# Z and gate columns of the second token half as seven block products on pairs of units

## The chip, the cores and the metric

The kernel runs on one core of one Trainium2 chip. The time is the device time of one execution in microseconds; three executions of a kernel give a median. A profile of one further execution gives the spans of all instructions and transfers. Engines are named as in the profile: PE (TensorE), DVE (VectorE), ACT (ScalarE), POOL (GpSimd), and SP (SyncE), which issues nearly all DMA transfers.

## What is computed

One hybrid decoder layer for 2048 tokens of 1024 channels: RMS norm, one input projection to 9224 columns, a gated DeltaNet branch and a dilated sliding-window attention branch, each with a SiLU gate path (the z columns), per-channel sigmoid gates, an output projection and the residual. Cut to what matters here:

```python
h = rms_norm(x, norm_w)
proj = h @ w_in                                  # (2048, 1024) @ (1024, 9224)
(dn_qkv, dn_z, dn_b, dn_a, swa_q, swa_k, swa_v, swa_z, gates) = split(proj)
o_dn  = rms_norm(delta_net(dn_qkv, dn_a, dn_b)) * silu(dn_z)      # 4 heads x 128
o_swa = merge(attention(swa_q, swa_k, swa_v)) * silu(swa_z)       # 4 heads x 128
g_dn, g_swa = split(gates)                                        # 2 x 1024
merged = sigmoid(g_dn) * (o_dn @ w_branch_dn) + sigmoid(g_swa) * (o_swa @ w_branch_swa)
out = x + merged @ w_out
```

The change concerns `swa_z` (512 columns) and `gates` (2048 columns) of `proj`.

## The kernel before

**Arithmetic.** Each float32 operand of a large product is split into a high part (rounded to fp32r, a copy on ScalarE) and a low part (the rest, a subtraction), and a product is three matmuls: high x high, high x low, low x high (`split`, line 86). The normalised input is held so in `hh` and `hl`, [128, 4, 8, 512]: four slots n of 512 tokens, eight slices k of 128 channels.

**First stage: attention columns.** The 4608 attention columns are computed for one token half (1024 tokens) at a time in 16 units (`unit`, line 413): units 0 to 7 for the first half, 8 to 15 for the second. A unit is a 2x2x2 block product (halves of the tokens, of the channels, of the unit's columns) done with seven block products in place of eight: `PROD` lists them, with the operand of x, the accumulator, whether it opens it, and the operand of w. The operands of x are the four blocks A11, A12, A21, A22 of the half and four sums of them: S1 = A21 + A22, S2 = S1 - A11, S3 = A11 - A21, S4 = A12 - S2; those of w are B11 to B22 and T1 = B12 - B11, T2 = B22 - T1, T3 = B22 - B12, T4 = T2 - B21. `SLOT` says where an operand of x stands: A11 to A22 of the half at hand in slots 2 and 3, the sums in slots 0 and 1. `save` and `restore` move an operand (high and low, 1 MB each) between its slot and the DRAM scratch `opd`; A11, A12 and A22 of the first half are saved in units 1 to 3, and during unit 15 the four blocks of the first half are loaded over the sums (`HOME`), so that afterwards `hh`, `hl` hold all 2048 tokens. The split w operands of the first half are written to `wdr` and read back for the second half. Attention runs meanwhile, a step every three or four hooks.

**Column blocks.** Then come 36 units of 128 columns each (`ccols`, line 1292): three z units of DeltaNet, twelve q, k, v units of DeltaNet, five z units (one of DeltaNet, four of `swa_z`), sixteen gate units. `cunits` (707) goes through them; for each it takes the four token slots n in turn, 24 matmuls of 128x512 into one bank of PSUM (three are there, `mm`), and gives the result to the unit's function: `z_block` (1145: tanh on ScalarE, a multiply on VectorE, store to `zscr`), `g_block` (1152: tanh, store to `gscr`) or a DeltaNet block. `c_load` (689) and `c_part` (703) fetch and split the next unit's w: high on ScalarE, low on GpSimd. The tiles `gt` of the z and gate functions are two.

**Work in the background.** `hook` (673) is called every six of these matmuls; `at(d, fn)` (670) puts a piece of work d hooks later. Pieces put there run beside the column blocks: after the first three units `open_dn` (1337); in unit 15, nine hooks in, `start_inverse` (1346): 63 rows of a triangular inverse on VectorE (`inverse`, 997; row i is one product of i x i elements, line 1020, and one reduction, 1023), each a number of hooks after the one before; then the store of the result, `scan` (1027; 16 steps of three hooks, with small matmuls on TensorE, each waiting for work of VectorE and ScalarE), then `start_fin` (1356: loads and merging of the attention outputs, `combine` 1186, and `o_prep` 1215). In the last unit, ahead of slot 2, `tail` (1377) starts loading and splitting the weights of the output projections into slots 0 and 1 of `hh`, `hl`.

**Order.** From `open_dn` to `start_inverse`, and all through the first stage, the order on PE, ACT, DVE and POOL is that of the program text (`manual_schedule`, line 1279); SP's is not, and elsewhere no engine's is: there a planner orders each engine's queue when the kernel is built, by its own estimate of when each instruction is ready, earlier ones in the text first. On the chip each queue is worked through in that order.

```python
PROD = (("A11", "a", True, "B11"), ("S2", "b", True, "T2"), ("A12", "a", False, "B21"), ("S3", "b", False, "T3"),
        ("S1", "c", True, "T1"), ("A22", "b", False, "T4"), ("S4", "c", False, "B22"))
SLOT = {"A11": (2, 0), "A12": (2, 1), "A21": (3, 0), "A22": (3, 1), "S1": (0, 0), "S2": (0, 1), "S3": (1, 0), "S4": (1, 1)}
```

## Time and profile before

| | |
|---|---|
| time, median of 3 runs | 2352.74 us (2350.87 to 2353.64) |
| the profiled execution | 2357.82 us |
| its span, first to last instruction | 2356.0 us |
| mean granted TensorE clock | 0.990 |
| DMA traffic | 452.23 MB, mean 192 GB/s |

How to read the profile: "busy" is the time in which an engine has at least one instruction running. Matmuls overlap, so the mean length of one in a group is longer than the distance between two; the distance comes from a count over a window in which TensorE does nothing else. A row of a group gives line, engine, operation, names written and read, shapes and count, then busy us and the mean ns of one, then the engine's idle time just before such instructions and who ended it. A row of a timeline gives start and length in us, and in brackets the idle time before it. A row of the chain gives start and length of a piece of the work that ended last. A row of DMA issues gives count, size and the median us from issue to landing. A row of windows gives for each stretch its length, each engine's busy us with the count, the granted clock, the DMA share and GB/s.

### The profile page before, as it was taken

The numbers are of one execution on the slowest core, as the hardware profiler recorded it, in microseconds if no ns is written. First come the engines' busy times: TensorE is split into PE (matmuls) and PEld (weight loads), VectorE is DVE, ScalarE is ACT, GpSimd is POOL, SyncE is SP. The second block draws the span as 40 slices with busy tenths as digits, with TensorE's granted clock in tenths as the row PEclk, the third lists the DMA queues.
The fourth block names the chain that finished last, engine by engine and source line by source line (L and its number), as shares of the span: only waits on it lengthen the run. The fifth ranks groups of instructions, "written<-read, shape, count | busy, mean of one in ns | idle before, by whom it ended". The sixth has DMA issues, their size and how long they took to land.

```text
span 2356.0 us, 43344 instructions
## 1 busy us (share of the span) xinstructions
PE 2297.1 (97%) x15216; PEld 2086.2 (89%) x15216; DVE 1347.7 (57%) x2853; ACT 907.2 (39%) x2948; POOL 889.2 (38%) x1331
## 2 busy tenths in 40 slices
PE   7999999979999999999999999999999999999999
PEld 7999999879999999888787888888888788889988
DVE  6566576594435535445777767999244423444431
ACT  5345466653324435445666651111233214111110
POOL 5374266574403303402675561111232213433442
PEclk8999999999999999999999999999999999999999
DMA  9989889857887888853544443222677636554542
GB/s 296 325 277 323 272 283 292 269 161 239 251 265 236 246 273 261 259 148 101 130 110 132 127 103 113 72 76 69 212 207 208 193 120 175 161 179 150 148 139 77
DMA packets 525969, 452.23 MB, mean 192 GB/s; under 512 B 66168, under 2 KB 490424, under 8 KB 523320
## 3 DMA queue, kind: packets, MB, share of 16 engines
q1 hardware_dynamic: 525464, 449.39, 62.6%
q8 instruction: 121, 1.98, 0.3%
q14 instruction: 96, 0.79, 0.1%
q10 hardware_dynamic: 288, 0.07, 0.0%
HBM read 263.45 MB, written 185.89 MB: 191 GB/s over the span
## 4 chain that ended last, share of the span: by engine, by line
PE 66%; DMA 5%; DVE 3%; POOL 1%; ACT 1%; issue 1%; SPq 0%; DVEq 0%; POOLq 0%; ACTq 0%
PE mm L433 12%; PE mm L720 10%; PE mm L721 10%; PE mm L722 10%; PE mm L1254 2%; PE mm L1256 2%; PE mm L1255 2%; PE mm L1237 2%; PE mm L1239 2%; PE mm L1238 2%; DMA oscr<-ol 2%; DMA gcb<-gcscr 1%; PE tp L584 1%; PE po L626 1%; DMA raw<-in_w_out_dram 1%; PE tp L617 1%
## 5 line engine op out<-in xcount | busy, mean ns | idle before, releaser
L720 PE MATMUL mm<-hh,w 128*128 128x512 f32 x1152 | 463.3, 402 | 0.0
L722 PE MATMUL mm<-hh,w 128*128 128x512 f32 x1152 | 457.8, 397 | 0.0
L721 PE MATMUL mm<-hl,w 128*128 128x512 f32 x1152 | 456.9, 397 | 0.0
L433 PE MATMUL mm<-w,hh 128*128 128x256 f32 x1760 | 328.3, 286 | 0.0
L433 PEld LDWEIGHTS mm<-w,hh 128*128 128x128 f32 x1760 | 271.2, 190 | 0.0
L88 POOL TENSOR_TENSOR w<-raw,w 128x512 fp32r<-128x512 f32 x68 | 100.0, 1472 | 435.0 <-ACT w L87 434.8
L720 PEld LDWEIGHTS mm<-hh,w 128*128 128x128 f32 x1152 | 220.3, 191 | 45.9
L722 PEld LDWEIGHTS mm<-hh,w 128*128 128x128 f32 x1152 | 217.0, 188 | 46.9
L433 PE MATMUL mm<-hh 128*128 128x256 f32 x880 | 257.5, 293 | 0.0
L721 PEld LDWEIGHTS mm<-hl,w 128*128 128x128 f32 x1152 | 217.6, 189 | 42.4
L433 PE MATMUL mm<-hl,hh 128*128 128x256 f32 x880 | 249.8, 284 | 0.9 <-POOL hl L295 0.9
L433 PE MATMUL mm<-hh,hl 128*128 128x256 f32 x880 | 249.6, 284 | 0.0
L433 PE MATMUL mm<-w,hl 128*128 128x256 f32 x880 | 248.3, 282 | 0.0
L607 DVE CUSTOM_DVE_ANT_0 p<-sc,mask 128x128 f32<-128x128 f32 (+1 forms) x192 | 70.0, 365 | 213.8 <-PE sc L604 87.0
L433 PEld LDWEIGHTS mm<-hl,hh 128*128 128x128 f32 x880 | 169.4, 192 | 1.3 <-POOL hl L295 1.3
L433 PEld LDWEIGHTS mm<-hh 128*128 128x128 f32 x880 | 169.3, 192 | 0.0
L433 PEld LDWEIGHTS mm<-hh,hl 128*128 128x128 f32 x880 | 169.0, 192 | 0.0
L433 PEld LDWEIGHTS mm<-w,hl 128*128 128x128 f32 x880 | 166.1, 189 | 0.0
L368 POOL TENSOR_SCALAR st<-st 128x4 f32<-128x4 f32 x96 | 21.1, 219 | 374.0 <-ACT junk L367 371.9
L1237 PE MATMUL mm<-oh,hh 128*128 128x256 f32 x512 | 143.7, 281 | 1.7 <-DVE gt L1241 1.7
L1239 PE MATMUL mm<-oh,hl 128*128 128x256 f32 x512 | 142.9, 279 | 0.0
L1238 PE MATMUL mm<-ol,hh 128*128 128x256 f32 x512 | 142.9, 279 | 0.0
(304 smaller groups left out, 5492.1 us busy)
## 6 DMA issues: line engine op xcount, KB each, us to landing
wdr<-w SPq DMA_DIRECT2D x56, 512.0 KB, 4.8
w<-wdr SPq DMA_DIRECT2D x54, 512.0 KB, 5.1
qk<-qks SPq DMA_DIRECT2D x212, 128.0 KB, 3.9
qks<-rec SPq DMA_DIRECT2D x96, 256.0 KB, 3.2
raw<-in_w_in_dram SPq DMA_DIRECT2D x68, 256.0 KB, 3.3
gscr<-gt SPq DMA_DIRECT2D x64, 256.0 KB, 2.5
gt<-gscr SPq DMA_DIRECT2D x64, 256.0 KB, 3.4
wdr<-hh SPq DMA_DIRECT2D x28, 512.0 KB, 4.4
```

Of the source, the lines that this page charges most:

```text
L88: eng.tensor_tensor(out=l, in0=raw, in1=h.bitcast(F32), op=ALU.subtract)
L433: mm = lambda x, y, **kw: nc.tensor.matmul(o, x, y, skip_group_check=True, **kw)
L607: nc.vector.tensor_tensor_reduce(out=p[:, lo:hi], in0=sc[:, lo:hi], in1=self.mask[:, slot * P + lo:slot * P + hi], scalar=3e38, scale=-SCA ...
L720: nc.tensor.matmul(pr, wh[:, k, :], a, start=(k == 0), stop=False)
L721: nc.tensor.matmul(pr, wh[:, k, :], b, start=False, stop=False)
L722: nc.tensor.matmul(pr, wl[:, k, :], a, start=False, stop=(k == KT - 1))
L1237: nc.tensor.matmul(o, self.wbh[:, k, ms], oh[:, k, :], start=(k == b * 4), stop=False)
L1238: nc.tensor.matmul(o, self.wbh[:, k, ms], ol[:, k, :], start=False, stop=False)
L1239: nc.tensor.matmul(o, self.wbl[:, k, ms], oh[:, k, :], start=False, stop=(k == b * 4 + 3))
L1254: nc.tensor.matmul(pr, mh[:, k, cs], self.woh[:, k, hs], start=(k == 0), stop=False)
L1255: nc.tensor.matmul(pr, mh[:, k, cs], self.wol[:, k, hs], start=False, stop=False)
L1256: nc.tensor.matmul(pr, ml[:, k, cs], self.woh[:, k, hs], start=False, stop=(k == KT - 1))
```

## The change

The units are put in another order: `ccols` now has the four z units of DeltaNet, twelve DeltaNet units (so `open_dn` and `start_inverse` come one unit later), four `swa_z` units (16 to 19) and sixteen gate units (20 to 35). `visits` lists the plain visits. Units 0 to 15 keep all four slots. Then unit 35 and units 17 to 34 are visited for the slots 0 and 1 alone, and unit 16 for all four. Ahead of slot 2 of unit 16 the sums S1 to S4 of the second token half, which units 9 to 12 have parked in `opd`, are loaded over slots 0 and 1 (`restore`). The nine `pairs` (17, 18) to (33, 34) then get their second token half from `s_pair`: seven products of 12 matmuls on two units' columns, in the order of `PROD`, in place of four blocks of 24. The intermediate sums are held in SBUF (`sh`); the outputs go to the same z and gate functions (`own`: the gate's tanh is done in place). `s_load` fetches the four w blocks of a pair, `s_ahead` makes and splits the w operands three products ahead into a ring of four entries in the tiles `wp0`, low parts on GpSimd for products 1, 3, 4, 5 and on VectorE for 0, 2, 6. Unit 35 gets its slots 2 and 3 at the end, after `tail`. The new tiles are in the pool `zp`; to make room, `cmask` moves from `sm` to `dp` and is loaded when that is opened. The diff, cut to its core:

```diff
@@ setup
-                    for p, op in ((0, "A11"), (0, "A12"), (0, "A21"), (0, "A22"), (1, "A21")) for x in range(2)}
+                    for p, op in ((0, "A11"), (0, "A12"), (0, "A21"), (0, "A22"), (1, "A21"), *((1, s) for s in HOME))
+                    for x in range(2)}
@@ unit
+        if 9 <= u < 13:
+            self.at(20, lambda: self.save(1, ("S1", "S2", "S3", "S4")[u - 9]))
@@ cunits
+        for v, n in [(0, 2), (1, 2), (0, 0), (1, 0), (0, 1), (0, 3), (1, 1), (1, 3)]:
+            self.c_block(v, n, fns)
...
+        last = len(self.visits) - 1
+        for v in range(2, last):
+            u = self.visits[v]
+            if v in pre:
+                pre[v]()
+            if u > 15 and v + 1 < last:
+                self.c_next(v + 1, (4, 6))
+            for n in range(NB if u <= 16 else 2):
+                if v == last - 1 and n == 2:
+                    for op in ("S2", "S3", "S1", "S4"):
+                        self.restore(1, op, *SLOT[op])
+                    self.s_load(0, ("B11", "B12", "B22", "B21"))
+                    for gi in range(2):
+                        self.at(3 + 2 * gi, lambda gi=gi: self.s_ahead(gi))
+                self.c_block(v, n, fns)
+                if n == 0 and v + 1 < last and u <= 15:
+                    self.c_next(v + 1, (4, 8))
+        self.s_ahead(2)
+        for q in range(len(self.pairs)):
+            self.s_pair(q, fns, last)
+        tail()
+        for n in (2, 3):
+            self.c_block(last, n, fns)
+
+    def s_ahead(self, gi):
+        q, i = divmod(gi, 7)
...
+        name = PROD[i][3]
+        if i == 1:
+            r[q, "T1"] = b11 = r.pop((q, "B11"))
+            sub(b11, r[q, "B12"], b11)
+            t2 = r[q, "T2"] = self.zp.tile([P, 4, P], F32, name="sraw", bufs=6)
+            sub(t2, r[q, "B22"], b11)
+        elif i == 3:
+            r[q, "T3"] = b12 = r.pop((q, "B12"))
+            sub(b12, r[q, "B22"], b12)
+        elif i == 5:
+            r[q, "T4"] = t2 = r.pop((q, "T2"))
+            sub(t2, r.pop((q, "B21")), t2)
+        h, l = self.s_entry(gi)
+        raw = r[q, name]
+        eng = self.nc.gpsimd if i in (1, 3, 4, 5) else V
+        d = 1 if i in (1, 3, 5) else 0
...
+    def s_pair(self, q, fns, last):
...
+        for i, (op, tgt, first, _) in enumerate(PROD):
+            gi = 7 * q + i
+            self.s_ahead(gi + 3)
+            if 2 <= i <= 4:
+                self.s_load(q + 1, (("B11",), ("B12", "B22"), ("B21",))[i - 2])
...
+            if first:
+                acc[tgt] = self.ps.tile([P, 512], F32, name="mm", bufs=3)
+            pr = acc[tgt]
+            ah, al = self.slot(op)
+            wh, wl = self.s_entry(gi)
+            for k in range(4):
+                mm = lambda x, y, **kw: nc.tensor.matmul(pr, x, y, skip_group_check=True, **kw)
+                mm(wh[:, k, :], ah[:, k, :], start=first and k == 0, stop=False)
+                mm(wh[:, k, :], al[:, k, :], start=False, stop=False)
+                mm(wl[:, k, :], ah[:, k, :], start=False, stop=(k == 3))
+                if k % 2:
+                    self.hook()
+            if i == 0:
+                hold["p1"] = new()
+                nc.scalar.activation(hold["p1"], pr, AF.Copy)
+            elif i in (1, 3):
+                n = "u2" if i == 1 else "u3"
+                hold[n] = new()
+                add(hold[n], pr, hold["p1"])
+            elif i == 2:
+                fns[self.pairs[q][0]](2, pr)
+            else:
+                n, tok, c = {4: ("u3", 1, 1), 5: ("p1", 1, 0), 6: ("u2", 0, 1)}[i]
+                o = self.gp.tile([P, 512], F32, name="gt", bufs=2)
+                add(o, pr, hold.pop(n))
+                self.at(1, lambda o=o, tok=tok, c=c: fns[self.pairs[q][c]](2 + tok, o, own=True))
@@ run
-        self.ccols = zc[:3] + dc + zc[3:] + gc
+        self.ccols = zc[:4] + dc + zc[4:] + gc
+        self.visits = [*range(16), 35, *range(17, 35), 16, 35]
+        self.pairs = [(u, u + 1) for u in range(17, 35, 2)]
```

111 lines of the change are left out of this document (73 added, 38 removed).

## The prediction

> **What bounds the kernel now.** I read the page first (busy shares, then the chain that ended last), then the windows of the stage that the change rewrites, then its groups of instructions and the timelines of VectorE and SyncE.
>
> ```profile
> PE 2297.1 (97%) x15216; PEld 2086.2 (89%) x15216; DVE 1347.7 (57%) x2853; ACT 907.2 (39%) x2948; POOL 889.2 (38%) x1331
> PE 66%; DMA 5%; DVE 3%; POOL 1%; ACT 1%; issue 1%; SPq 0%; DVEq 0%; POOLq 0%; ACTq 0%
> L720 PE MATMUL mm<-hh,w x1152: 388/389/776, 979.4 to 1975.5; 128*128 128x512 f32 x192
> 1450.00:1650.00 200.00, 200.00 (x867) 163.70 (x866) 194.85 (x200) 31.96 (x54) 32.25 (x18) 1.00 0.24 74
> 1696.00:1848.00 152.00, 152.00 (x1090) 134.26 (x1089) 66.43 (x219) 57.55 (x236) 47.84 (x153) 1.00 0.68 197
> 1856.00:1976.00 120.00, 116.09 (x502) 94.77 (x501) 36.87 (x74) 27.94 (x52) 19.97 (x20) 0.97 0.51 155
> ```
>
> TensorE is busy 97% of the span and is two thirds of the chain. The stage of the change runs from 979.4 to 1975.5. The last three rows are windows in it (columns: length, then PE, PEld, DVE, ACT, POOL busy with counts, clock, DMA share, GB/s): the triangular inverse on VectorE (1450 to 1650), the scan (1696 to 1848) and the start of the last stage (1856 to 1976). TensorE does not idle in the first two. So a matmul taken away is time taken away, as long as the queues beside it keep up.
>
> In 1450 to 1650 all 867 matmuls are 128x512 ones of the column blocks, so one costs 200 / 867 = 0.2307 us (its row says 389 ns, but they overlap). A block of 24 takes 5.54 us, a product of 12 takes 2.77, a hook (6 matmuls) 1.384. Note the VectorE there: 194.85 of 200 us busy.
>
> **What the change removes.** Eighteen units lose their two second-half blocks (36 blocks, 864 matmuls), and nine pairs get 63 products of 12 (756). That is 108 matmuls fewer: 108 x 0.2307 = **24.9 us**, if nothing waits.
>
> **What it adds, where it is hidden.**
>
> ```profile
> L87 ACT ACTIVATE w<-raw 128x512 fp32r<-128x512 f32 x18 | 11.4, 633 | 36.9 <-PE mm L721 36.9
> L88 POOL TENSOR_TENSOR w<-raw,w 128x512 fp32r<-128x512 f32 x18 | 33.8, 1883 | 168.3 <-ACT w L87 168.3
> L1149 DVE SCALAR_TENSOR_TENSOR gt<-gt,mm 128x512 f32<-128x512 f32 x13 | 8.9, 681 | 0.0
> L1155 ACT ACTIVATE gt<-mm 128x512 f32<-128x512 f32 x24 | 14.3, 595 | 87.3 <-PE mm L722 64.0 <-issue 23.3
> ```
>
> Per pair (7 x 2.77 = 19.4 us): VectorE gets four subtractions, three low parts and five additions, 12 x 0.68 = 8.2 us; ScalarE seven high parts (0.63), a copy and four tanh (0.60), 7.4 us; GpSimd four low parts, 4 x 1.88 = 7.5 us. All are under half of a pair, and entries are made three products (8.3 us) ahead, against 0.68 + 0.63 + 1.88 = 3.2 us: hidden behind the products, as long as VectorE is not held by something else. Uncovered, every such entry would cost up to its 3.2 us. The tight places are three evictions with only one product (2.77 us) between them and the matmul that overwrites or continues their bank: u2 before product 3, u3 before product 5, the addition of product 4 before product 6. The plain visits are halved to 11.1 us each; their 2 x (0.63 + 1.88) us of splitting and 0.5 MB of loads fit in that.
>
> **Term 1: the inverse's last rows are in front of the first pair.**
>
> ```profile
> 1415.62 0.28 DVE L994 COPY nbt<-tp 64x128 f32<-64x128 f32 x1
> 1429.36 7.55 DVE L1005 TENSOR_TENSOR M<-Z,nb 128x4096 f32<-128x4096 f32 x1 [2.35 <-DMA Z<-lscr]
> 1436.83 0.67 DVE L1149 SCALAR_TENSOR_TENSOR gt<-gt,mm 128x512 f32<-128x512 f32 x1
> ...
> 1636.89 4.16 DVE L1020 TENSOR_TENSOR Z<-M 128x3844 f32<-128x3844 f32 x1
> 1645.32 5.09 DVE L1020 TENSOR_TENSOR Z<-M 128x3969 f32<-128x3969 f32 x1
> 1650.52 4.23 DVE L1023 TENSOR_REDUCE M<-Z 128x63 f32<-128x3969 f32 x1
> 1654.81 2.02 DVE L1015 COPY Z<-M 128x2048 f32<-128x2048 f32 x1
> 1686.71 0.43 DVE L1061 TENSOR_TENSOR zs<-sc,nbr 64x256 f32<-64x256 f32 x1 [29.88 <-PE sc L1058]
> ```
>
> The inverse starts nine hooks into a visit (the copy at 1415.62) and its rows end at 1654.8, 239 us later. In the new order the visits end 168 hooks after the visit's start, so the first pair starts 159 hooks, 159 x 1.384 = 220 us, after the same point. Four z evictions fewer (-2.7 us) and low part 0, T1 and T2 (+2) leave the rows' end near 238: rows 62 and 63 (8.4 and 9.4 us) stand beside the pair's first products. In program order row 62 comes just ahead of the subtractions T1 and T2, and row 63 ahead of u2. Without a wait product 3 would start at 220 + 3 x 2.77 = 228.3; with u2 behind row 63 it starts at 239.7: **11.4 us**, or 8.6 if product 4, which needs neither, is put ahead of it. Both ends: 0 (u2 gets between the rows) and 15 (T2's low part at GpSimd's pace comes on top). I take 9. Behind the waiting u2 on VectorE stand T4 and the next low parts. The scan does not suffer: the 29.88 us that VectorE sat idle before it, after the inverse, are its slack.
>
> An idle TensorE then runs slow for a while:
>
> ```profile
> 1884.62 1.09 PE L1221 MATMUL tp<-ident,osw 128*128 128x128 f32 x4 [3.91 <-DVE osw L1206]
> ```
>
> After that idle time of 3.91 us the window 1856 to 1976 has a granted clock of 0.97: 0.03 x 120 = 3.6 us lost. Ends: 0 and 3.6; I take 2.5. The Trainium skill (TensorE: Matmul & The Clock Gate, Part 1: The HAM clock gate) says that one idle window of about 3.4 us halves the clock until a busy one has passed, which as an estimate would be 1.7 us; the row shows about twice that, and by the page the sum would be 0.8 us better.
>
> **Term 2: eight saves of 1 MB, units 9 to 12.**
>
> ```profile
> 540.00:560.00 20.00, 20.00 (x171) 20.00 (x171) 1.58 (x3) 3.95 (x16) 2.32 (x3) 1.00 0.95 298
> 980.00:990.00 10.00, 8.56 (x45) 6.96 (x43) 4.82 (x14) 3.31 (x12) 6.76 (x17) 1.00 0.99 388
> 542.64 58.46 PE mm L433 x492
> w<-wdr SPq DMA_DIRECT2D x54, 512.0 KB, 5.1
> qk<-qks SPq DMA_DIRECT2D x212, 128.0 KB, 3.9
> raw<-in_w_in_dram SPq DMA_DIRECT2D x68, 256.0 KB, 3.3
> cmask<-in_cmask_dram SPq DMA_DIRECT2D x1, 64.0 KB, 2.7
> 649.18 2.13 PE mm L433 x18
> 652.08 2.12 PE mm L433 x18
> 557.95 2.03 SPq L697 DMA_DIRECT2D wr<-in_w_in_dram  x4
> 1865.90 4.03 SPq L1175 DMA_DIRECT2D raw<-in_w_branch_swa_dram  x3
> ```
>
> SyncE does not keep program order: the loads at 557.95 have their place at the last two products ahead of the stage that starts at 979.4, those at 1865.90 two blocks before 1975.5. So the saves will go as soon as the sums are there, near 545, and not at their place. At 388 GB/s (the window with four 1 MB restores) 8.39 MB take 21.6 us, in a stretch whose DMA share is 0.95. Weights for a product (48 x 58.46 / 492 = 5.7 us) are fetched three products ahead: 17.1 - 5.1 = 12 us of cover. Spread among those loads the saves cost nothing, in one lump about 10 us. I take 2, near the lower end, since weight loads come first in program order and get in between.
>
> **Term 3: eight restores and the pair's weights.** By the same rule the weights of pair 0 (no operand holds them back) load long before, and S2 and S1 once block 0 of the last full visit is done. Even from the end of block 1 the four land at about 7, 13, 18 and 24 us (5.4 each, 1.5 to start); they are needed at 13.9, 19.4, 22.2 and 27.7 (11.1 for two blocks, then products 1, 3, 4 and 6). Cost 0; the other end is a rival.
>
> **Moved, at no cost.** One z unit goes ahead of the twelve DeltaNet units with its instructions unchanged. The load of cmask moves behind the attention's end on SyncE's queue, in front of the gcb loads; its reader comes ten hooks (13.8 us) later and it lands in 2.7, which is also its price uncovered. Inverse, scan and first outputs need 269 hooks from the visit in which the inverse starts; 302 are left there where 336 were.
>
> **Term 4: scan, its loads, and the merging of the attention outputs.**
>
> ```profile
> L1118 DVE TENSOR_SCALAR os<-qs,oss 128x128 f32<-128x128 f32 x60 | 16.5, 316 | 35.7 <-POOL oss L1116 35.7
> L1091 PEld LDWEIGHTS tp<-rr,vb 128*128 128x128 f32 x113 | 14.9, 190 | 1.9 <-DVE rr L1084 0.8
> 1879.09 4.05 DVE L1203 TENSOR_TENSOR oc<-oc,cs 128x512 f32<-128x512 f32 x3
> ```
>
> In the scan TensorE never idles, but the weights that VectorE makes for it come just in time (L1091 waits 0.8 us on rr), and rr stands behind os, which waits for GpSimd. The scan's 48 hooks now cross 3.4 pairs, with 14 low parts on GpSimd and 41 more VectorE operations. Ends: 0 and 14 x 0.5 = 7 us; I take 2. The stores of the first pairs stand on SyncE's queue with the scan's loads: 0 to 5, I take 1. The merging (4.05 us in one go) stands in front of additions with 2.77 us of cover: 0 to 6, I take 0.5 beyond the 3.91 us already lost there.
>
> **Sum.** -24.9 + 9 + 2.5 + 2 + 0 + 2 + 1 + 0.5 = **-7.9 us**. The profiled execution took 2357.8 us (span 2356.0); taken to the median of the runs, 2352.7 - 7.9 = 2344.8, I say 2345.
>
> **The rivals.**
>
> *Nothing waits.* VectorE's queue lets T1, T2 and u2 in between the rows. For it: B's loads are early, and rows leave gaps. Against: in 1450 to 1650 VectorE is 97% busy, and the z eviction at 1436.83 had to sit out the 7.55 us operation in front of it. -24.9 plus 5 for the rest: 2333.
>
> *The saves go out in one lump (slower).* Place: unit 8, near 550. 21.6 us of backlog against 12 us of cover stalls TensorE about 10 us, the clock takes up to 3.6 more, and the attention's loads (three steps ahead, a step every 2.9 us by the rows at 649.18 and 652.08, 3.9 to land, so 4.8 us of cover) wait a few us more until the backlog has drained: 16 in place of 2, so 2359. It decides from a cost of 12.6 us on (7.9 + 4.7). For it: the low-priority loads at 557.95 show SyncE free there. Against: the share of 0.95 leaves the planner little room for a lump.
>
> *The pair's weights queue behind the restores.* If SyncE keeps program order there, B11 lands 1.5 + 21.6 + 3.3 us after block 1 and its parts are ready 1.3 us later, at 27.7, against 11.1 of cover; T2 adds 2.5. The 19 us replace term 1's 9: 2355.
>
> *The pairs do not run faster.* If the three tight evictions cost 0.9 us each, a pair takes the 22.1 us of its eight blocks: the 24.9 are gone and the rest of the costs stays, near 2368. Against: 8.2 us of VectorE work in 19.4.
>
> **How the numbers follow.** Forecast 0.43 (2339 to 2351), nothing waits 0.25, lump 0.15, weights behind restores 0.10, no faster pairs 0.07. A measurement of this kernel tells about 0.2% (4.7 us) from no change. Faster: three quarters of the forecast and all of the second case, 0.58. Slower: the lump and the slow pairs, 0.20 with their neighbours' tails. Same: 0.22. The range 2329 to 2360 takes in the first three cases and the fourth.
>
> **What would show it.** The column blocks and products together have 3348 matmuls in place of 3456. From the second pair on outside the scan seven products take 19.4 us. In the first pair TensorE idles some 9 us on VectorE, with row 63 just ahead of u2. The saves are issued near 545; no idle time of over 3 us on weights follows. The pair's first weights land long before the restores. I am wrong if the first pair does not wait, if the stretch from 540 to 980 grows by more than 5 us, or if the later pairs take over 21 us.

## The result: slower by 0.87%

| | before | after |
|---|---|---|
| time, median | 2353.64 us (2350.87 to 2357.44, 5 runs) | 2373.69 us (2372.65 to 2379.41, 5 runs) |
| ratio, after to before | | 1.0087, 95% interval 1.0074 to 1.0101 |
| span of the profiled execution | 2356.0 us | 2371.5 us |
| mean granted TensorE clock | 0.990 | 0.987 |

The forecast was 2345 us, with a range of 2329 to 2360. The change costs 20 us where 8 were to be gained. The matmuls did go: this is the profile after, the page's first line and the groups of the column blocks, then the groups of the products between 1661 and 1980 (line, engine, operation, names, shapes, count; busy us, mean ns; idle time in front).

```profile
PE 2285.4 (96%) x15108; PEld 2069.0 (87%) x15108; DVE 1429.7 (60%) x2961; ACT 950.3 (40%) x3022; POOL 955.1 (40%) x1369
L721 PE MATMUL mm<-hh,w 128*128 128x512 f32 x864 | 344.5, 399 | 0.0
L723 PE MATMUL mm<-hh,w 128*128 128x512 f32 x864 | 343.0, 397 | 0.0
L722 PE MATMUL mm<-hl,w 128*128 128x512 f32 x864 | 342.2, 396 | 0.0
```

```profile
L831 PE MATMUL mm<-hh,w 128*128 128x512 f32 x504 | 178.4, 417 | 17.8 <-DVE gt L1265 5.0 <-DVE gt L813 3.5 <-ACT w L797 3.1
L831 PE MATMUL mm<-hl,w 128*128 128x512 f32 x252 | 102.7, 407 | 0.0
```

3 x 864 + 504 + 252 = 3348 matmuls, 108 fewer than 3 x 1152. But TensorE idles 17.8 us in front of the products, and VectorE, ScalarE and GpSimd are busy 82, 43 and 66 us longer than before.

Where the time went is read from windows cut at the stage's seams. Columns: length, PE, PEld, DVE, ACT, POOL busy (count), granted clock, DMA share, GB/s. First the attention units 8 to 15 before the change, then the stages after it: the same units, then (behind the plain blocks) pair 0, pair 1, pair 2, pairs 3 to 5 (all beside the scan), pairs 6 to 8.

```profile
542.50:979.40 436.90, 428.17 (x3612) 425.64 (x3610) 207.45 (x697) 181.98 (x772) 127.37 (x274) 0.99 0.83 257
```

```profile
538.30:983.50 445.20, 431.07 (x3612) 426.23 (x3611) 207.85 (x697) 182.82 (x772) 127.02 (x274) 0.99 0.85 269
...
1661.60:1694.00 32.40, 24.35 (x85) 17.23 (x84) 28.26 (x25) 8.38 (x9) 9.93 (x3) 0.84 0.75 282
1694.00:1734.20 40.20, 31.88 (x176) 25.66 (x174) 19.69 (x37) 12.88 (x34) 12.53 (x23) 0.96 0.59 164
1734.20:1753.70 19.50, 19.50 (x84) 15.98 (x85) 9.30 (x15) 8.36 (x16) 4.79 (x4) 1.00 0.62 184
1753.70:1906.50 152.80, 149.87 (x1034) 129.52 (x1033) 85.73 (x241) 66.04 (x243) 57.39 (x153) 0.99 0.71 202
1906.50:1978.20 71.70, 66.02 (x295) 52.80 (x294) 51.62 (x97) 26.43 (x57) 25.49 (x26) 0.98 0.59 181
```

The attention units grew by 8.3 us. Pair 2, beside which little else runs, takes 19.5 us, the 7 x 2.77 that were forecast. Pair 0 takes 32.4: TensorE is idle for 32.4 - 24.35 = 8.05 us of it, and at a granted clock of 0.84 loses 0.16 x 32.4 = 5.2 more. The rest of the loss is not yet visible in these rows, since pairs 1 and 3 to 8 have other work of TensorE between their products; the experiments have to separate it.

How pair 0 waits is seen in four timelines (start, length; in brackets the idle time in front and who ended it), of VectorE, of TensorE, of ScalarE and of GpSimd.

```profile
1662.93 4.15 DVE L1136 TENSOR_TENSOR Z<-M 128x3844 f32<-128x3844 f32 x1
...
1667.68 4.10 DVE L1139 TENSOR_REDUCE M<-Z 128x62 f32<-128x3844 f32 x1
1671.70 0.68 DVE L778 TENSOR_TENSOR sraw<-sraw 128x512 f32<-128x512 f32 x1
...
1672.31 0.68 DVE L800 TENSOR_TENSOR w<-sraw,w 128x512 fp32r<-128x512 f32 x1
1672.91 4.29 DVE L1136 TENSOR_TENSOR Z<-M 128x3969 f32<-128x3969 f32 x1
1677.11 0.68 DVE L813 TENSOR_TENSOR sh<-mm,sh 128x512 f32<-128x512 f32 x1
...
1677.79 4.23 DVE L1139 TENSOR_REDUCE M<-Z 128x63 f32<-128x3969 f32 x1
```

```profile
1673.04 0.73 PE L831 MATMUL mm<-hh,w 128*128 128x512 f32 x2 [2.16 <-DVE w L800]
...
1683.37 0.47 PE L831 MATMUL mm<-hh,w 128*128 128x512 f32 x1 [2.37 <-DVE gt L1265]
...
1686.39 0.80 PE L831 MATMUL mm<-hh,w 128*128 128x512 f32 x1 [2.32 <-ACT w L797]
```

```profile
1682.05 3.78 ACT L1130 ACTIVATE Z<-M 128x2048 f32<-128x2048 f32 x1 [0.57 <-DVE M L1138]
1685.72 0.62 ACT L797 ACTIVATE w<-sraw 128x512 fp32r<-128x512 f32 x1
```

```profile
1659.25 1.30 POOL L800 TENSOR_TENSOR w<-sraw,w 128x512 fp32r<-128x512 f32 x1 [25.54 <-ACT w L797]
1665.07 3.18 POOL L800 TENSOR_TENSOR w<-sraw,w 128x512 fp32r<-128x512 f32 x1 [4.52 <-ACT w L797]
1673.18 5.16 POOL L800 TENSOR_TENSOR w<-sraw,w 128x512 fp32r<-128x512 f32 x1 [4.94 <-ACT w L797]
```

A low part on VectorE (1672.31) comes only behind the reduction of row 62, and TensorE waits 2.16 us for it; u2 (the `sh` at 1677.11) does get in between row 63's product and its reduction; a z eviction and a sum stand behind that reduction, and TensorE waits again, 2.37 us. The third wait, 2.32 us, ends with a high part that ScalarE makes at 1685.72: that part stood behind ScalarE's half of the copy of the inverse's result, which began as soon as row 63 was done and took 3.78 us. GpSimd is held as well: two of its low parts end at 1668.25 and 1678.34, some 1.2 us after the rows' products on VectorE end (1662.93 + 4.15 = 1667.08 and 1672.91 + 4.29 = 1677.20); the one at 1659.25, which meets a row's reduction and no product, takes 1.30 us.

### The profile page after: what moved, and what is told of

Same layout as the page of the kernel before. It is cut to its first block, busy times and chain, and to the rows that moved or that the text cites. A ratio compares the mean times of both kernels' runs of the same rounds, so it can differ in the third digit from the quotient of the medians.

```text
span 2371.5 us, 43564 instructions
## 1 busy us (share of the span) xinstructions
PE 2285.4 (96%) x15108; PEld 2069.0 (87%) x15108; DVE 1429.7 (60%) x2961; ACT 950.3 (40%) x3022; POOL 955.1 (40%) x1369
## 3 DMA queue, kind: packets, MB, share of 16 engines
q8 instruction: 120, 1.97, 0.3%
## 5 line engine op out<-in xcount | busy, mean ns | idle before, releaser
L721 PE MATMUL mm<-hh,w 128*128 128x512 f32 x864 | 344.5, 399 | 0.0
L723 PE MATMUL mm<-hh,w 128*128 128x512 f32 x864 | 343.0, 397 | 0.0
L722 PE MATMUL mm<-hl,w 128*128 128x512 f32 x864 | 342.2, 396 | 0.0
L89 POOL TENSOR_TENSOR w<-raw,w 128x512 fp32r<-128x512 f32 x70 | 110.9, 1587 | 304.7 <-ACT w L88 304.5
L831 PE MATMUL mm<-hh,w 128*128 128x512 f32 x504 | 178.4, 417 | 17.8 <-DVE gt L1265 5.0
L721 PEld LDWEIGHTS mm<-hh,w 128*128 128x128 f32 x864 | 164.8, 191 | 33.3
L723 PEld LDWEIGHTS mm<-hh,w 128*128 128x128 f32 x864 | 162.5, 188 | 35.0
L722 PEld LDWEIGHTS mm<-hl,w 128*128 128x128 f32 x864 | 162.7, 188 | 32.2
```

The lines of the kernel that those rows point to most:

```text
L89: eng.tensor_tensor(out=l, in0=raw, in1=h.bitcast(F32), op=ALU.subtract)
L721: nc.tensor.matmul(pr, wh[:, k, :], a, start=(k == 0), stop=False)
L722: nc.tensor.matmul(pr, wh[:, k, :], b, start=False, stop=False)
L723: nc.tensor.matmul(pr, wl[:, k, :], a, start=False, stop=(k == KT - 1))
L831: mm = lambda x, y, **kw: nc.tensor.matmul(pr, x, y, skip_group_check=True, **kw)
```

## The experiments

Times are given as the ratio to the kernel before, measured in the same job, since its median moved between 2353 and 2357 us from job to job. "Against after" is (ratio - 1.0087) x 2354 us; by the two intervals it is uncertain by some 4 us, so small differences between runs mean little. Lengths of stages are from one profile each.

| run | ratio (95% interval) | against after, us | units 8 to 15, us | first to last column block, us |
|---|---|---|---|---|
| before | 1 | | 436.9 | 996.5 |
| after | 1.0087 (1.0074 to 1.0101) | | 445.2 | 1005.6 |
| no saves | 1.0055 (1.0042 to 1.0068) | -7.5 | 433.1 | 1007.7 |
| no last rows | 1.0011 (1.0001 to 1.0021) | -17.9 | 446.6 | 984.9 |
| weights of pair 0 only | 1.0011 (0.9999 to 1.0024) | -17.9 | 450.1 | 982.6 |
| all three left out | 0.9910 (0.9896 to 0.9925) | -41.7 | 436.7 | 973.5 |
| order of units undone | 1.0062 (1.0045 to 1.0079) | -5.9 | 444.0 | 1002.3 |
| z pairs last | 1.0044 (1.0029 to 1.0059) | -10.1 | 448.7 | 1001.4 |
| both orders | 1.0070 (1.0055 to 1.0085) | -4.0 | 444.7 | 1003.7 |
| low parts on DVE | 1.0070 (1.0053 to 1.0087) | -4.0 | 445.9 | 1005.9 |
| six pairs | 1.0130 (1.0115 to 1.0145) | +10.1 | 450.0 | 1013.6 |
| six pairs, text's order | 1.0226 (1.0209 to 1.0243) | +32.7 | 445.8 | 1042.8 |
| four pairs | 1.0029 (1.0015 to 1.0044) | -13.7 | 450.1 | 992.0 |
| saves spread, from ACT | 1.0144 (1.0129 to 1.0160) | +13.4 | 455.0 | 1008.2 |
| fourth save in unit 10 | 1.0098 (1.0081 to 1.0115) | +2.6 | 448.8 | 1005.3 |
| saves called in unit 15 | 1.0111 (1.0094 to 1.0128) | +5.6 | 442.9 | 1014.6 |
| that and both orders | 1.0093 (1.0077 to 1.0108) | +1.4 | 440.8 | 1011.3 |
| saves whole, from ACT | 1.0125 (1.0107 to 1.0142) | +8.9 | 454.6 | 1007.9 |

### What is left out: three costs and a gain

**The inverse's last rows.**

```diff
-            V.tensor_tensor(out=pr, in0=M[:, 0:i, 0:i], in1=M[:, i, 0:i].unsqueeze(1).to_broadcast([P, i, i]), op=ALU.mult)
+            if i < 60:
+                V.tensor_tensor(out=pr, in0=M[:, 0:i, 0:i], in1=M[:, i, 0:i].unsqueeze(1).to_broadcast([P, i, i]), op=ALU.mult)
...
-            V.tensor_reduce(out=M[:, 0:i, i:i + 1], in_=pr, axis=mybir.AxisListType.X, op=ALU.add)
+            if i < 60:
+                V.tensor_reduce(out=M[:, 0:i, i:i + 1], in_=pr, axis=mybir.AxisListType.X, op=ALU.add)
```

> The inverse's rows 60 to 63 (their product and their reduction, some 33 us of DVE) are left out; every other instruction and the places at which they are issued stay. Theory A (these rows on DVE cost pair 0 its 13 us and part of pair 1's delay): pair 0 takes 20 to 22 us in place of 32.4, and the time falls by 13 to 22 us. Theory B (the pair is bound by its own evictions through two output tiles, or by loads): pair 0 stays above 28 us, and the time falls by less than 5 us. Theory C (the delay is handed on): pair 0 is 20 to 22 us, but the time falls by less than 8 us, pair 1 and the scan's start then being longer.

Measured: 17.9 us less. The windows of pairs 0 and 1 in this kernel, and GpSimd's group in its pair 0, then the same group in the changed kernel's pair 0:

```profile
1663.10:1682.50 19.40, 19.40 (x86) 15.87 (x84) 9.19 (x14) 6.52 (x11) 5.41 (x4) 1.00 0.97 373
1682.50:1717.10 34.60, 29.81 (x176) 24.64 (x174) 15.81 (x33) 11.33 (x31) 10.29 (x22) 1.00 0.84 236
```

```profile
L800 POOL TENSOR_TENSOR w<-sraw,w 128x512 fp32r<-128x512 f32 x4 | 5.4, 1353 | 23.6 <-ACT w L797 23.6
```

```profile
L800 POOL TENSOR_TENSOR w<-sraw,w 128x512 fp32r<-128x512 f32 x3 | 9.9, 3311 | 17.5 <-ACT w L797 17.5
```

Rows 60 to 63 are left out here. Theory A holds. Pair 0 takes 19.40 us with TensorE busy throughout, in place of 32.4, though the 8 MB of restores and the next pair's weights pass beside it (DMA share 0.97): the restores cost nothing there. Pair 1 falls by 5.6 us as well, so the delay did go on into it. Without the rows a low part takes GpSimd 1.35 us on the mean, with them 3.31. The Trainium skill (SBUF — State Buffer, Who interferes with whom) says that a VectorE instruction with two SBUF inputs contends with a GpSimd instruction that reads SBUF, and calls the contention an exclusive lock; the ends at 1668.25 and 1678.34 agree, each some 1.2 us behind the end of a row's product.

**The weights of the pairs.**

```diff
 def s_load(self, q, names):
-        if q == len(self.pairs):
+        if q >= 1:
             return
...
 def s_ahead(self, gi):
-        if q == len(self.pairs):
+        if q >= 1:
             return
```

> The weights of pairs 1 to 8 are left out: no loads, no sums on DVE, no high parts on ACT, no low parts on GpSimd or DVE; these pairs multiply by the operands of pair 0. Their products, their sums of products and their stores stay. Theory A (preparing the pairs' weights takes DVE, ACT and GpSimd time that the scan needs): the products of pairs 3 to 5, which run beside the scan, fall from some 7.25 us to 6.9, pair 1 falls from 40 us to 30 or less, and the time falls by 12 to 20 us. Theory B (the loss lies in the evictions and in the order behind the inverse's last rows): pair 1 stays above 36 us and the time falls by less than 6 us. Pair 0 is 32 us by both.

Measured: 17.9 us less. Pairs 1, 3 to 5 and 6 to 8 in this kernel (windows), then VectorE's group `os` (the scaling of the scan's outputs) beside the scan in the changed kernel and in this one, and what TensorE's weight loads waited for in the changed kernel:

```profile
1694.10:1730.60 36.50, 31.81 (x190) 26.36 (x188) 10.72 (x28) 8.04 (x27) 3.19 (x10) 1.00 0.66 184
...
1750.10:1893.90 143.80, 143.80 (x1022) 126.32 (x1020) 67.90 (x216) 52.93 (x215) 37.89 (x134) 1.00 0.64 188
1893.90:1959.30 65.40, 63.32 (x295) 51.86 (x294) 37.22 (x89) 16.72 (x40) 11.02 (x15) 1.00 0.58 177
```

```profile
L1234 DVE TENSOR_SCALAR os<-qs,oss 128x128 f32<-128x128 f32 x55 | 17.4, 358 | 30.8 <-POOL oss L1232 30.8
```

```profile
L1234 DVE TENSOR_SCALAR os<-qs,oss 128x128 f32<-128x128 f32 x54 | 13.0, 284 | 31.9 <-POOL oss L1232 31.9
```

```profile
PEld tp L1207 <- DVE rr L1200: 5.8, 9, 1.5
```

Theory A in the main. Pairs 3 to 5 fall by 9.0 us, to 143.8 with no idle time; pairs 6 to 8, beside which the attention outputs are merged and transposed, by 6.3; pair 1 by 3.7, to 36.5, not to 30. In the changed kernel TensorE waits for rr (an operand of the scan that VectorE makes), and os, behind which rr stands, takes 358 ns on the mean in place of 284; in this kernel TensorE's weight loads wait for rr no longer. The loads of these weights are left out with them, so what the loads alone cost is not separated. Which part of the 9.0 us is VectorE's and which GpSimd's was tried by moving four low parts of seven from GpSimd to VectorE, from pair 2 on:

```diff
-        eng = self.nc.gpsimd if i in (1, 3, 4, 5) else V
+        eng = self.nc.gpsimd if q < 2 and i in (1, 3, 4, 5) else V
```

> The low parts of the pairs' weights that GpSimd makes (four of seven, 1.32 us each beside the scan) are made by DVE instead from pair 2 on (0.69 us each); pairs 0 and 1 stay. Theory A (in the scan DVE's os waits behind GpSimd's chain, that behind the low parts, and rr behind os): pairs 3 to 5 fall from 152.8 us to 145 to 149, and the time by 4 to 9 us. Rival B (DVE's own queue is what rr stands in, and more work on DVE makes it worse): pairs 3 to 5 rise to 154 or more, and the time rises by 0 to 6 us. Pairs 0 and 1 are the same by both.

Measured: pairs 3 to 5 took 150.9 us, 1.9 less, between the two theories, and the intervals of the ratios overlap (1.0053 to 1.0087, 1.0074 to 1.0101). Nothing follows for the time; moving these four parts changes little.

**The saves.**

```diff
-        if 9 <= u < 13:
-            self.at(20, lambda: self.save(1, ("S1", "S2", "S3", "S4")[u - 9]))
...
-                        self.restore(1, op, *SLOT[op])
+                        self.restore(0, HOME[op], *SLOT[op])
```

> The four saves of the second half's parked sums (eight transfers of 1 MB) are left out; the restores read blocks of the same size that the first half stored, so the gate and z columns of the second half are not those of the reference. All else is the same. Theory A (the saves cost the 7.4 us by which units 8 to 15 of the attention stage grew, by traffic): units 8 to 15 take 435 to 437 us in place of 443.3, and the time falls by 6 to 9 us, to 2365 to 2368. Rival (the growth comes from the order of the instructions or from a difference between profiles): units 8 to 15 stay at 441 us or more and the time falls by less than 3 us.

Measured: 7.5 us less, units 8 to 15 in 433.1 us:

```profile
539.40:972.50 433.10, 425.45 (x3612) 422.78 (x3611) 207.24 (x697) 182.49 (x772) 127.30 (x274) 1.00 0.84 260
```

Theory A as to the size. Over all profiles: nine kernels that call the saves as the change does took 444.0 to 450.1 us there (mean 446.8); the three without saves 433.1 to 436.9 (mean 435.6). The difference of 11.2 us is more than the timed 7.5. More than half of it (6.3 us by the means) stands in one place: unit 12 takes 63.4 to 66.0 us in the nine, and 58.0 to 59.7 in the three.

**All three at once** (the three edits above in one kernel).

> Three things are left out together: the saves of the second half's parked sums (the restores read first-half blocks of the same size), the inverse's rows 60 to 63 on DVE, and the weights of pairs 1 to 8 (they multiply by pair 0's). Theory A (three separate costs stand over a gain of 24.9 us from 108 matmuls fewer, and the cost of the rows and of the weights overlap by the 6 us that pairs 0 and 1 gained by either): 2354.7 - 24.9 = 2330, at most 5 us above it. Rival (there is a fourth cost, of the reordered units or of the half visits, or the matmuls bring less): 2338 or more.

Measured: 2332.3 us, ratio 0.9910. Theory A: 41.7 us against the changed kernel, where the three alone gave 7.5 + 17.9 + 17.9 = 43.3. The gain is then 0.0090 x 2354 = 21.2 us of the 24.9, and there is no large fourth cost: the reordered units, the half visits and the restores together cost some 3.7 us (0.4 to 7.2 by the interval). Its pair 0 and its pairs 3 to 5, with TensorE busy throughout:

```profile
1653.40:1672.80 19.40, 19.40 (x86) 15.88 (x85) 5.43 (x8) 4.72 (x8) 6.19 (x11) 1.00 1.01 420
...
1728.50:1871.50 143.00, 143.00 (x1014) 125.87 (x1013) 67.49 (x215) 53.10 (x215) 38.03 (x134) 1.00 0.63 188
```

### Can order alone take the costs away?

**The order of the units undone**, so that the inverse starts one unit sooner against the pairs.

```diff
-        self.ccols = zc[:4] + dc + zc[4:] + gc
+        self.ccols = zc[:3] + dc + zc[3:] + gc
...
-        self.cunits(zu[:4] + du + zu[4:] + gu, {4: open_dn, 16: lambda: self.at(9, start_inverse)}, tail)
+        self.cunits(zu[:3] + du + zu[3:] + gu, {3: open_dn, 15: lambda: self.at(9, start_inverse)}, tail)
```

> The order of the units goes back to that of before (the fourth z unit behind the twelve units of the second layer's keys, queries and values), so that the inverse starts one full unit, some 22 us, sooner against the pairs; nothing else changes. Theory A (pair 0 loses 13 us because its z sums and evictions stand among the inverse's rows 60 to 63 on DVE, and hands the delay on to pair 1, where the scan starts): the rows are done before the first pair, pair 0 takes 20 to 23 us in place of 32.4, and the time falls by 10 to 20 us, to 2354 to 2364. Theory B (the pairs themselves are short of DVE, of ACT or of the two output tiles wherever z and gate columns are evicted): pair 0 stays above 28 us, and the time within 4 us of 2373.7. Theory C (the pairs merely move their loss: what is late at pair 0 is late at the scan's start): pair 0 falls to some 20 us, but pair 1 and the scan's start grow by as much, and the time stays within 5 us of 2373.7.

Measured: 5.9 us less, with intervals that just touch. Pair 0 falls to 26.3 us, between the theories, and pair 1, which now holds the scan's start from its first product on, rises to 41.5. Part of the delay is handed on, as C said, though less than all of it: the two pairs together are 4.8 us shorter. What TensorE mostly waits for between 1660 and 1730 here:

```profile
PE mm L831 <- ACT w L797: 7.5, 2, 4.3
```

**The pairs with z columns last.**

```diff
-        self.pairs = [(u, u + 1) for u in range(17, 35, 2)]
+        self.pairs = [(u, u + 1) for u in (*range(21, 35, 2), 17, 19)]
```

> The same nine pairs in another order: the seven of g columns first, the two with z columns last. A z block takes one more operation of DVE (0.68 us) and one more of the two output tiles than a g block. Theory A (the extra operation and tile, in front of which TensorE waited 2.4 and 2.7 us, are part of what pairs 0 and 1 lose): pair 0 falls from 32.4 us to 26 to 29, pair 1 from 40 to 36 to 38, and the time by 4 to 9 us. Rival (the low parts, the sums and the adds behind rows 62 and 63 alone set it): pair 0 stays above 30 us and the time within 3 us of 2373.7.

Measured: 10.1 us less. Its pairs 0, 1 and 2:

```profile
1666.70:1699.60 32.90, 24.85 (x86) 17.93 (x85) 28.77 (x25) 9.95 (x12) 9.72 (x3) 0.84 0.76 288
1699.60:1728.30 28.70, 28.14 (x166) 23.52 (x164) 10.00 (x19) 9.34 (x27) 8.70 (x15) 1.00 0.65 179
1728.30:1751.20 22.90, 20.88 (x95) 16.66 (x94) 16.71 (x26) 10.12 (x19) 9.73 (x12) 1.00 0.76 210
```

Pair 0 is as long as ever, so its loss does not come from z columns (the rival was right there). Pairs 1 and 2 together take 51.6 us in place of 59.7.

**Both orders together.**

> Two changes of order together: that of the units as before the change (the inverse starts 22 us sooner against the pairs), and the two pairs with z columns last. Theory A (the two gains of 6 and 8.5 us have causes of their own): 2358 to 2361. Rival (both move the scan's start against the same pair, so that they share a gain): 2364 to 2368.

Measured: 4.0 us less, no better than either alone (5.9 and 10.1), and above the time that the rival gave. Pairs 0 and 1 took 28.0 and 41.0 us. The two gains do not add; that both come from the place of the scan's start against the pairs, as the rival says, fits this but is not shown.

**Six pairs**, units 17 to 22 as plain blocks, so that the last rows and the scan's first preparations stand beside plain blocks.

```diff
-        self.visits = [*range(16), 35, *range(17, 35), 16, 35]
-        self.pairs = [(u, u + 1) for u in range(17, 35, 2)]
+        self.visits = [*range(16), 35, *range(23, 35), *range(16, 23), 35]
+        self.pairs = [(u, u + 1) for u in range(23, 35, 2)]
...
-            for n in range(NB if u <= 16 else 2):
+            for n in range(NB if u <= 22 else 2):
```

> Only units 23 to 34 are made as pairs (six); units 17 to 22 have their four blocks as plain blocks, and so the inverse's last rows and the scan's preparation fall beside plain blocks, as before the change. 36 matmuls of 0.23 us come back (8.3 us). Theory A (pairs are dear where the inverse's last rows hold DVE): the first pair takes 20 us outside the scan or some 50 inside it, without a stall of its own, and the time is 2373.7 - 18.8 + 8.3 = 2363, or less by what the weights of three pairs cost (7 us): 2356 to 2363. Rival (the delay belongs to the first pairs wherever they stand, through the restores, the weights or the two output tiles): the first two pairs again lose 15 us or more, and the time is 2373 to 2385.

Measured: 10.1 us more, which is the rival's number and not theory A's. The rows disturb no pair any longer, but pairs 0 to 2, all beside the scan, take 170.6 us where pairs 3 to 5 of the changed kernel took 152.8 for as many instructions of TensorE (1034). The window, and what TensorE waited for most in it:

```profile
1743.50:1914.10 170.60, 153.34 (x1034) 131.46 (x1032) 87.00 (x238) 67.71 (x245) 55.09 (x152) 0.95 0.69 193
```

```profile
PE sc L1182 <- DVE zs L1177: 9.1, 9, 2.1
PE sc L1174 <- DMA t<-tscr: 4.9, 2, 3.2
```

In this kernel's queue of TensorE the scan's matmuls stand in clumps, with hardly a product between them and the step of VectorE that they wait for:

```profile
1787.79 0.45 PE L1174 MATMUL sc<-t,lo 64*64 64x64 f32 x5
1788.17 0.49 PE L831 MATMUL mm<-hh,w 128*128 128x512 f32 x1
1789.83 0.67 PE L1182 MATMUL sc<-vb,zs 64*64 64x64 f32 x8 [1.16 <-DVE zs L1177]
```

I took that for the planner's doing and kept the text's order there (`manual_schedule` from the first pair to the last, SP left free):

```diff
-        for q in range(len(self.pairs)):
-            self.s_pair(q, fns, last)
+        with self.pinned(False):
+            for q in range(len(self.pairs)):
+                self.s_pair(q, fns, last)
```

> The kernel with six pairs (2383.7 us), but from the first pair to the last the order on PE, ACT, DVE and GpSimd is that of the program text, where the planner chose it. In the planner's order of that kernel the scan's products stand in clumps without a pair's matmuls between them, and TensorE waited 9.1 us for zs on DVE, 4.9 us for loads and 3.2 us for w on ACT in the first three pairs, which took 170.6 us. Theory A (the planner's order made the scan dear there): these pairs fall to some 150 us, and the time by 15 to 22 us. Rival (it is the place of the pairs against the scan, or the 8 MB of restores at its start): they stay above 165 us, and the time within 5 us of 2383.7. A third way (the text's order is worse, because each half step's chain PE, DVE, PE has only one hook of cover): 175 us or more.

Measured: 22.6 us more than the six pairs, and pairs 0 to 2 took 199.6 us. That is the third way: the text's order is worse, and that the planner chose badly is not shown. Why the scan and the pairs get in each other's way more in this place than in the other stays open.

**Four pairs**, units 27 to 34, behind the scan, in the unit order of before (the first edit of this section) and with the fourth save in unit 10 (an edit shown further below):

```diff
-        self.visits = [*range(16), 35, *range(17, 35), 16, 35]
-        self.pairs = [(u, u + 1) for u in range(17, 35, 2)]
+        self.visits = [*range(16), 35, *range(27, 35), *range(16, 27), 35]
+        self.pairs = [(u, u + 1) for u in range(27, 35, 2)]
...
-            for n in range(NB if u <= 16 else 2):
+            for n in range(NB if u <= 26 else 2):
```

> Pairs only for units 27 to 34 (four), behind the scan; units 16 to 26 have four plain blocks, the order of the units is that of before, and the fourth save stands in unit 10. So the inverse's rows, the scan's start and nearly all of the scan run beside plain blocks. Theory A (a pair gains its 2.77 us wherever DVE, ACT and GpSimd have room for its weights, and pairs beside the last rows or the scan give the gain back): 2354 - 11.1 + 0 to 2 for the saves + 4 to 7 around the output's transposes = 2345 to 2351. Rival B (the saves and restores eat what four pairs bring, wherever they stand): 2352 to 2358. Rival C (plain blocks in the planner's new order lose beside the scan, as the six pairs did): 2360 or more.

Measured: 2362.1 us, ratio 1.0029, the best of the kernels that leave nothing out, and still slower than before. From the first to the last column block it took 992.0 us, 4.5 less than before the change; 11.1 were to be had from 48 matmuls fewer, and its first pair, at the end of the scan, took 28.9. Units 8 to 15 took 450.1. The time lies in C's range, but the plain blocks ahead of the pairs lose nothing: they take 888.4 us, and as many column-block matmuls took 888.7 before the change. By mechanism B is nearest: four pairs bring less than the saves cost.

### Is there a place where the saves are free?

The two transfers of the fourth save are issued at 766.8 and 767.3 in the changed kernel, in unit 12, which takes 65.3 us there and 58.0 without saves. So that save was moved:

```diff
-        if 9 <= u < 13:
-            self.at(20, lambda: self.save(1, ("S1", "S2", "S3", "S4")[u - 9]))
+        if 9 <= u < 12:
+            self.at(20, lambda: self.save(1, ("S1", "S2", "S3")[u - 9]))
+        if u == 10:
+            self.at(44, lambda: self.save(1, "S4"))
```

> The save of the fourth parked sum is called in unit 10 (hook 44) in place of unit 12 (hook 20); the other three stay, and so do the bytes. In the profiles of the change and of the kernel without saves, 7.3 of the 12.1 us between them stand in unit 12 (65.3 against 58.0 us), where the two transfers of this save were issued, near 767. Theory A (these two alone collide with the attention's loads there; units 8 to 11 keep TensorE busy and bear 2 MB more): unit 12 takes 57 to 60 us, and the time falls by 5 to 8 us, to 2366 to 2369. Rival (any 8 MB cost this stage the same wherever they stand): unit 12 falls, units 10 or 11 grow by as much, and the time stays within 2.5 us of 2373.7.

Measured: nothing gained (2.6 us more, intervals overlapping). Unit 12 fell by 2.6 us, unit 11 rose by 4.2. That this save makes unit 12 long was a wrong reading: in the changed kernel TensorE's longest wait in that unit ends at 762.37, before the save is issued, and in the four kernels that issue no save there (this one, the four pairs and the two that call the saves in unit 15) unit 12 still takes 61.6 to 63.7 us, against 58.0 to 59.7 without saves.

Next the bytes were cut into 32 pieces of 256 KB, issued by ScalarE every sixth hook of units 9 to 12:

```diff
-            self.at(20, lambda: self.save(1, ("S1", "S2", "S3", "S4")[u - 9]))
+            for j in range(8):
+                self.at(4 + 6 * j, lambda j=j: self.save_part(("S1", "S2", "S3", "S4")[u - 9], j // 4, j % 4))
...
+    def save_part(self, op, x, k):
+        self.nc.scalar.dma_start(dr(self.opd[1, op, x], 512 * k, [[2048, P], [1, 512]]), self.slot(op)[x][:, k, :].bitcast(F32))
```

> The eight saves of 1 MB are cut into 32 of 256 KB, and issued by ACT one by one, every sixth hook of units 9 to 12, in place of by SP in lumps; the bytes are the same. Theory A (the saves cost their 7.5 us as lumps that push weight loads back some 3 us each): units 8 to 15 fall from 445 us to 435 to 439, and the time by 4 to 8 us. Rival (this stage is short of DMA bandwidth, so that 8 MB cost what they cost wherever they stand): units 8 to 15 stay at 442 us or more and the time within 3 us of 2373.7. A second rival (ACT's queue is held by the issues): units 9 to 12 grow, others do not.

Measured: 13.4 us more, 455.0 us for the units. Theory A falls, and so does the first rival, by which the time would have stayed. Units 10 and 11 grew most (59.6 and 62.8 us, 56.1 and 57.1 in the changed kernel), which is the second rival's place; unit 12, of which it said the same, did not grow (62.8 in place of 65.3).

Then the saves were called in the last unit, each ahead of the load that overwrites its operand:

```diff
-        if 9 <= u < 13:
-            self.at(20, lambda: self.save(1, ("S1", "S2", "S3", "S4")[u - 9]))
...
                 if op in HOME:
+                    self.save(p, op)
                     self.restore(1 - p, HOME[op], *SLOT[op])
```

> The four saves stand in the last unit (15), each behind the last product that reads its operand and ahead of the load that overwrites it; the bytes are the same. So units 8 to 14 carry no save, and 8 MB more pass between some 930 and 1000, beside the last attention and the first plain blocks, where the share of the DMA engines is 0.7 to 0.9 before 1000 and 0.3 to 0.6 behind it. Theory A (the saves cost what they delay in the attention's own loads, and there is a place beside which nothing waits): units 8 to 14 fall to the 370.7 us that they take without saves, the first plain blocks lose at most 3 us, and the time falls by 4 to 8 us. Rival (8 MB cost some 8 us wherever they stand): the last unit and the first blocks grow by 6 us or more, and the time is 2371 to 2378.

Measured: 5.6 us more (the intervals overlap). This run did not test what it was to test: SP's queue is ordered by the planner, and three of the four saves went out early all the same, as six transfers between 529.67 and 600.60. The first and the last of them in SP's timeline:

```profile
529.67 0.33 SPq L103 DMA_DIRECT2D opd1S<-hh  x1
...
600.60 0.43 SPq L103 DMA_DIRECT2D opd1S<-hl  x1
```

The one save that did stand at the end (issued at 971.9 and 982.6) seems to be paid in the plain blocks, where the first block to the last took 9.0 us more. With both orders besides:

> Both orders and the late saves in one kernel. If each has its gain by itself: 2373.7 - 6 - 8.5 - 6 = 2353, the time of the kernel before within 3 us; if the late saves bring nothing, 2358 to 2361; if the two orders share theirs too, 2364 or more. By none of them is it faster than before by more than 4 us, since the pairs' weights beside the scan (some 18 us) stay.

Measured: 2378.5 us, the last of the three cases: the orders share their gain, and the late call of the saves brings nothing. Last, the saves went whole into ScalarE's queue, which keeps the text's order here, in units 11 to 14:

```diff
-        if 9 <= u < 13:
-            self.at(20, lambda: self.save(1, ("S1", "S2", "S3", "S4")[u - 9]))
+        if 11 <= u < 15:
+            self.at(20, lambda: self.save(1, ("S1", "S2", "S3", "S4")[u - 11], self.nc.scalar))
...
-            self.nc.sync.dma_start(self.opd_ap(p, op, x), t.bitcast(F32))
+            (eng or self.nc.sync).dma_start(self.opd_ap(p, op, x), t.bitcast(F32))
```

> The four saves, whole (eight transfers of 1 MB), are issued from ACT's queue at hook 20 of units 11 to 14. ACT keeps the order of the text in this stage, so they cannot go out sooner than there; SP's plan put three of the four between 530 and 602 whether the text called them in units 9 to 11 or in unit 15. Theory A (the cost is the lump in units 8 and 9: 6 MB within 72 us, and what SP's later loads and stores inherit from it): units 8 to 15 fall from some 447 us (mean of the kernels with this lump) to 440 or less, and the time by 5 us or more. Theory B (8 MB cost this stage some 11 us wherever they stand): units 8 to 15 stay at 444 to 449 us, with the growth in units 11 to 14, and the time within 3 us of 2373.7. Theory C (an issue from ACT delays the attention's softmax, as the spread saves did): above 450 us.

Measured: 8.9 us more, units 8 to 15 in 454.6 us, of which unit 11, where the first one now stands (issued at 703.2 and 708.2), took 66.6 in place of 57.1. Theory A's time did not come: with no save ahead of 703 the stage is not shorter. It meets C's number, but whether the issues on ScalarE or the transfers themselves make unit 11 wait, this run can't tell, nor what the early lump would cost without that. That the saves cost this stage 7 to 11 us is shown, and that unit 12 bears more than half of it; by which wait is not.

## Why the prediction was wrong, step by step

| step | predicted, us | measured, us |
|---|---|---|
| 108 matmuls fewer | -24.9 | -21.2 (all three left out) |
| term 1, rows and clock | 9 + 2.5 | 17.9 (13.0 in pair 0, 5.6 in pair 1 by the profiles) |
| term 2, saves | 2 | 7.5 |
| term 3, restores and first weights | 0 | 0 |
| term 4, scan, stores, merging | 2 + 1 + 0.5 | 17.9 for the pairs' weights (the stores alone were not measured) |
| shared by the three costs | | -1.6 (43.3 one by one, 41.7 together; inside the noise) |
| sum | -7.9 | +20 |

**What bounds the kernel** was right: a matmul taken away is time taken away, as long as the queues keep up. With the three costs left out, 21.2 of the 24.9 us are there (17.7 to 24.5 by the interval; in the profiles the column blocks are 23.0 us shorter). Where the rest went was not traced.

**Term 1** had the right place and nearly the right size for pair 0: 11.5 predicted, 13.0 measured, by idle time (8.05) and clock (5.2) in other shares. The order was not the one I gave: u2 did not stand behind row 63, the low part of product 2 stood behind row 62, and a z eviction and a sum behind row 63. So that pair 0's total nearly agrees is partly luck. Three things were left out. GpSimd's low parts take 3.31 us on the mean, not 1.88, beside rows of this size. ScalarE's copy of the inverse's result holds a high part back (the third wait). And the delay does not end with the pair: "the scan does not suffer" was said of the scan, whose slack is real, but pair 1's first two products then took 3.93 and 6.95 us in place of 2.77 each, 5.3 of its 5.6. (A slip that changes little: row 63's end near 238.5 and u2's 0.68 give 239.2, not 239.7.)

**Term 2 was mis-sized.** Between its ends, 0 and 10, I took 2 "near the lower end", because weight loads would get in between the saves. They did: three saves went out between 531 and 602 and the fourth at 767, TensorE was busy 20 of 20 us in each of the windows 540 to 560 and 560 to 580, and no wait on weights appeared, so the lump rival fell. I am wrong, I wrote, if the stretch from 540 to 980 grows by more than 5 us. It grew by 8.3, in the attention's part of it, which I had priced only in the rival.

**Term 3** held: the four loads of the first weights went out at 1453.6, the restores from 1642.2 on, and beside the restores pair 0 runs in 19.4 us once the rows are gone. (From 5.4 each and 1.5 to start the landings are 6.9, 12.3, 17.7 and 23.1, up to 0.9 sooner than written; no row gives the 1.5.)

**Moved, at no cost** held within the 3.7 us that are not traced. That the inverse starts a unit later is part of why its last rows stand beside pair 0, which is term 1.

**Term 4 is the step that failed most.** A mechanism was named (rr behind os behind GpSimd) and the scan was given 0 to 7 us, with 2 taken; leaving the weights out brought 9.0 in pairs 3 to 5. The 0.5 us per low part behind the 7 is an estimate that no row gives. Beside the merging and the transposes I took 0.5 out of 0 to 6, and pairs 6 to 8 fell by 6.3. Beside the scan's start nothing was priced, and pair 1 fell by 3.7. The step that misled was "hidden behind the products", from shares "under half of a pair": these are averages over engines taken as free, and beside the scan, its start and the merging they are not.

**The rivals.** "The pairs do not run faster" came nearest by time (2368; its terms add up to between 2369 and 2370), by the wrong mechanism: the tight evictions cost nothing, pair 2 takes 19.5 us. No rival had the terms all at their upper ends, which comes near what was measured: 15 + 3.6 + 10 + 7 + 5 + 6 - 24.9 = +21.7. The range should have reached there.

## What to carry to other kernels

A cheaper product on the bounding engine is worth its gain less what its operands cost on the other engines in the same stage: nine pairs gained some 21 us and their weights took back 18, though no other engine was busy for more than 60% of the span. Read the cover of each added operation from the window in which it will run (who holds VectorE there, what does GpSimd's operation last beside it), not from averages. When a term's ends are 0 and 10 and the mechanism is in the trace, take the middle at least, and leave one kernel with all costs left out for the test of the sum: here it closed to 2 us in 42, inside the noise.

## What the runs showed of the hardware

**Half a window of idle time is enough to halve TensorE's clock.** The granted clock changes at seams 3.41 us apart. Windows of the changed kernel cut at these seams, each pair or triple without a gap:

```profile
1670.29:1673.70 3.41, 1.25 (x6) 0.72 (x5) 3.41 (x5) 0.63 (x1) 0.52 (x1) 1.00 0.93 316
1673.70:1677.11 3.41, 3.41 (x9) 2.15 (x7) 3.41 (x1) 0.30 (x1) 3.41 (x1) 0.50 0.05 14
...
1840.96:1844.37 3.41, 1.97 (x17) 1.65 (x16) 2.40 (x7) 2.12 (x7) 0.28 (x2) 1.00 0.49 93
1844.37:1847.78 3.41, 3.41 (x12) 2.75 (x11) 0.79 (x2) 0.91 (x3) 0.00 (x0) 0.50 0.94 310
1939.94:1943.35 3.41, 1.86 (x9) 1.21 (x8) 3.31 (x8) 1.11 (x2) 1.60 (x2) 1.00 0.68 194
1943.35:1946.77 3.42, 1.54 (x10) 1.06 (x9) 3.15 (x7) 0.63 (x1) 0.79 (x1) 1.00 1.01 293
1946.77:1950.18 3.41, 3.41 (x10) 2.64 (x9) 2.23 (x4) 1.26 (x2) 2.10 (x2) 0.50 1.02 328
```

Windows busy for 1.25, 1.54 and 1.97 us are each followed by one at 0.50; the one busy for 1.86 is not, so the border is not sharp. Over the traces of all eighteen kernels, behind the first 60 us and cut at their seams, all 124 windows at full clock with less than 1.5 us busy are followed by one at 0.50, 24 of the 120 with 1.5 to 2.0 us, and 3 of the 277 with 2.0 to 2.6. The Trainium skill (TensorE: Matmul & The Clock Gate, Part 1: The HAM clock gate) lets the clock fall after an idle window; none of the windows shown was idle, and the rows decide. Three stalls of 2.2 to 2.4 us cost pair 0 three windows at half clock, 3 x 1.7 = 5.1 us, where the forecast had 2.5 for one long stall.

**An operation of GpSimd can take four times its length beside VectorE**: 5.16 us for a low part that takes 1.35 without the rows. It started at 1673.18, while a row's product with both operands in SBUF ran on VectorE (1672.91 to 1677.20), and ended 1.14 us behind it.
